# Split weight blocks 544 bytes apart, with three buffer pairs at three places mod 256

## The chip, the cores and the metric

The kernel runs on one core of one Trainium2 chip. The metric is the device time in microseconds of one execution, as the median of several runs. The profile is one further execution, recorded by the hardware profiler; its span is the time from the first to the last instruction.

## What is computed

One step of a layer of a hybrid decoder, for 1024 prompt tokens and 8 sample tokens (1032 columns) and a width of 2048, in float32. Cut to what matters:

```python
h = rmsnorm(x, g_pre)
proj = h @ w_in                                   # 2048 x 10240
q, k, v, za, ub, zb, ga, gb = split(proj)
ya = (retention(q, k, v) * silu(za)) @ w_pa
yb = s5(ub); yb = yb * sigmoid(yb @ w_glu + b_glu)
yb = (yb * silu(zb)) @ w_pb
out = (sigmoid(ga) * ya + sigmoid(gb) * yb) @ w_out
return x + rmsnorm(out, g_post), states
```

Nearly all of the arithmetic is in the products with `w_in`, `w_pa`, `w_pb`, `w_glu` and `w_out`.

## The kernel before

**Split operands.** Both operands of the large products are float32 and are split into a high and a low part of type float32r: high is a cast on ScalarE, low is what the cast left over, a subtraction on VectorE. A product of two split operands is three matmuls: high by high, high by low, low by high (weight named first). Function `three` does this in the first stage, `product` (line 924) in the others.

**Products.** After the first stage the large products are done by a scheme with seven products of half-size blocks instead of eight. A step is one pair of output rows; its seven products use sums and differences of weight blocks (`prep`) and of moving blocks (the forms, which are made earlier and laid into the tiles `a0` to `a15`). One product has four pieces i = 0 to 3 of 128 contraction rows. In the stages up to the output, a moving piece has 516 columns, taken as 256 and 260, so a product is 4 pieces x 3 terms x 2 = 24 matmuls. In the two output stages (`o0`, `o1`) the piece has 324 columns and a product 12 matmuls. There are 90 steps with 24 matmuls a product and 16 steps with 12.

**The stages in order.** First the columns for the S5 branch and the first rows of v, by `linear` and `three`, with moving slices of 384 and 264 columns (lines 218 to 220); then the steps over `w_in`, with the S5 branch and the retention as background work on the other engines; then `glu`, `pa`, `pb`, `o0`, `o1`; last the first 384 tokens of the output product in a form where the weights are the moving operand, 512 columns wide (line 1755).

**Buffers of the split weights.** `wpair` hands out three pairs of buffers in turn, (`whia`, `wloa`), (`whib`, `wlob`), (`whic`, `wloc`). Each is a tile of 520 float32 words, 2080 bytes, of which 512 words are used: four blocks of 128 columns, 512 bytes apart. `prep(g + 2)` casts and subtracts the weights of the product after the next (lines 905 and 85), then the 24 matmuls of product g follow. The pair is free again when the product that used it has ended, so ScalarE waits for TensorE before each cast.

**Places.** A matmul's weight block and its moving piece each start at some byte of a partition. As the pools are laid out, the starts of the tiles mod 256 are:

| tile | start mod 256 before |
|---|---|
| whib, wlob | 160, 192 |
| whic, wloc | 224, 0 |
| whia, wloa | 32, 64 |
| a0, a1, a2, a3, ... | 96, 160, 224, 32, ... (8256 bytes each, 64 mod 256) |

In a moving tile (`qslot`) piece i has its high part at 4128 x (i mod 2) bytes and its low part 2064 bytes behind, so from piece to piece the start moves by 32 mod 256, also across two tiles, and the low part is 16 above the high one. The weight block moves by 512 bytes from piece to piece, 0 mod 256. With the form number the start of the first moving piece alternates between 96 and 224. In the output stages the pieces are 2592 bytes apart and the low part 1296 behind, again 32 and 16 mod 256.

**Smaller tiles that the change touches.** `rms_bcast` (line 269) spreads a row of factors over all partitions by matmuls with a 128x128 tile of ones. `s5_toep` and `s5_states` use small tiles from a pool (`dti`, and `x1` with two buffers). `ret_const` has a tile `selr`, `head` a tile `ons`.

Of the kernel before, what the change touches and what calls it, by code (L numbers as in the profile page):

```python
# [10 lines left out]
F32 = mybir.dt.float32  # L11
F32R = mybir.dt.float32r
I32 = mybir.dt.int32
AF = mybir.ActivationFunctionType
ALU = mybir.AluOpType
# [3 lines left out]
D = 2048  # L19
SEQ = 1024  # L20
NB = 8
# [58 lines left out]
def emit(ctx, tc, I, O):  # L80
    nc = tc.nc
    V, A, P, T = nc.vector, nc.scalar, nc.gpsimd, nc.tensor
# [12 lines left out]

    const = ctx.enter_context(tc.tile_pool(name="const", bufs=1))
    wp = ctx.enter_context(tc.tile_pool(name="wp", bufs=3))
    stage_of = {}

    def stage_pool(w, bufs):  # L100
# [53 lines left out]
        A.dma_start(t, I[name] if src is None else src)  # L154
        return t

    ones = const.tile([128, 128], F32, name="ones")
    onesk = const.tile([128, 1], F32, name="onesk")
    V.memset(onesk, 1.0 / D)
    V.memset(ones, 1.0)  # L160
    rstd = const.tile([128, TOK], F32, name="rstd")
    warm = const.tile([128, 1], F32, name="warm")
    A.activation(warm, onesk, AF.Square)
# [1 line left out]
    ident = cload("ident", [128, 128])  # L165
# [27 lines left out]
        return wtile(wd[m, :, 4 * kq:4 * kq + 4, :])  # L193

    pair_n = [0]

    def wpair():
        n = pair_n[0] = (pair_n[0] + 1) % 3
        return [wp.tile([128, 520], F32R, name=f"{x}{'abc'[n]}", bufs=1)[:, 0:512].rearrange("p (a b) -> p a b", a=4)
                for x in ("whi", "wlo")]  # L200

    def wtile(src):
        turn[0] += 1
        n = turn[0] % (3 + len(more))
        if "pool" in raw_of:
            raw = raw_of["pool"].tile([128, 4, 128], F32, name="wr")
        else:
            raw = more[n] if n < len(more) else wp.tile([128, 4, 128], F32, name="wraw")
        anchor["s"] = nc.sync.dma_start(raw if len(src.shape) == 3 else raw.rearrange("p a b -> p (a b)"), src).ins
        hi, lo = wpair()  # L210
        anchor["a"] = A.copy(hi, raw).ins
        anchor["v"] = sub(lo, raw, hi.bitcast(F32)).ins
        return hi, lo
# [55 lines left out]
    def rms_bcast(ssq, out, pool, extra=None):  # L269
        n = out.shape[-1]  # L270
        chunks = [(c, min(c + 128, n)) for c in range(0, n, 128)]
        nch = len(chunks)
        ps = misc()
        for i, (a, b) in enumerate(chunks):
            T.matmul(ps[0:b - a, i:i + 1], ssq[:, a:b], onesk, start=True, stop=extra is None)
            if extra is not None:
                T.matmul(ps[0:b - a, i:i + 1], extra[:, a:b], onesk, start=False, stop=True)
        ms = pool.tile([128, 9], F32, name="ms")
        rs = pool.tile([128, 9], F32, name="rs")
        hf = pool.tile([128, 9], F32, name="hf")  # L280
        V.memset(ms, 1.0)
        V.memset(hf, -0.5)
        r = chunks[-1][1] - chunks[-1][0]
        full = nch if r == 128 else nch - 1
        V.tensor_scalar(ms[:, 0:full], ps[:, 0:full], EPS, None, ALU.add)
        if full < nch:
            V.tensor_scalar(ms[0:r, full:nch], ps[0:r, full:nch], EPS, None, ALU.add)
        P.tensor_tensor(rs[:, 0:nch], ms[:, 0:nch], hf[:, 0:nch], ALU.pow)
        yield
        for i in range(0, nch, 4):  # L290
            pb = misc()
            for jj in range(i, min(i + 4, nch)):
                a, b = chunks[jj]
                r = b - a
                dg = st_tile()[:, 0:128]
                V.tensor_scalar(dg[0:r, 0:r], ident[0:r, 0:r], rs[0:r, jj:jj + 1], None, ALU.mult)
                T.matmul(pb[:, a - i * 128:b - i * 128], ones[0:r, :], dg[0:r, 0:r], start=True, stop=True)
            a, b = chunks[i][0], chunks[min(i + 4, nch) - 1][1]
            V.tensor_copy(out[:, a:b], pb[:, 0:b - a])

# [98 lines left out]
    def s5_params():  # L399
# [114 lines left out]
        for i in range(10):  # L514
            if i:
# [17 lines left out]


    FIXED = {"E": (14, 0), "rt": (14, 512), "W1": (14, 1024), "Tm": (14, 1536), "mA": (15, 0), "mB": (15, 576),
             "Z": (15, 1088), "zz": (15, 1632), "b2": (15, 1744), "B2": (15, 1808), "bt": (15, 1872), "cp": (15, 1936)}
    whole = {}

    def W(name, shape, bufs=1):
# [115 lines left out]
    def s5_states(b):  # L655
        g0 = 4 * b
        q0 = 2 * b
        pp = s5p
        d = s5d[b]
        W1, U, E, rt = d["W1"], d["U"], d["E"], d["rt"]  # L660
        X = d["X"] = W("X", [128, 4, 137])
        P.dma_start(X[:, :, 0:8], I["x0s"][:, g0:g0 + 4, :])
        P.memset(X[:, :, 8:9], 0.0)
        x0 = W("x0", [128, 2, 2, NB], 2)
        P.dma_start(x0, I["x0p"][:, :, q0:q0 + 2, :])
        Vc = W("Vc", [128, 2, 2, 144])
        for e in range(2):
            ps = misc()
            for q in range(2):
                g = 2 * q + e  # L670
                T.matmul(ps[:, q * 144:(q + 1) * 144], W1[:, g, :], U[:, g, :], start=True, stop=True)  # L671
            pv = ps[:, 0:288].rearrange("p (q c) -> p q c", q=2)
            A.copy(Vc[64 * e:64 * e + 64, 0], pv[0:64])
            A.copy(Vc[64 * e:64 * e + 64, 1], pv[64:128])
        v = Vc[:, :, :, 8:136]
        Erb = E[:, 0:1].broadcast_to([128, 2, 2, 128])
        Eib = E[:, 1:2].broadcast_to([128, 2, 2, 128])
        mA = W("mA", [128, 2, 2, 128])
        mB = W("mB", [128, 2, 2, 128])
        Z = W("Z", [128, 2, 2, 128])  # L680
        fl = lambda t: t.rearrange("p r q c -> p (r q c)")
        yield
        mul(mA, v, Erb)
        mul(mB, v, Eib)
        add(mA[:, 0], mA[:, 0], mB[:, 1])
        sub(mA[:, 1], mA[:, 1], mB[:, 0])
        V.tensor_tensor_scan(fl(Z), fl(rt), fl(mA), 0.0, op0=ALU.mult, op1=ALU.add)
        yield
        mul(mA, Z, Erb)
        mul(mB, Z, Eib)  # L690
        Xv = X.rearrange("p (q e) c -> p e q c", e=2)
        for e in range(2):
            h_ = slice(64 * e, 64 * e + 64)
            sub(Xv[0:64, e, :, 9:137], mA[h_, 0], mB[h_, 1])
            add(Xv[64:128, e, :, 9:137], mA[h_, 1], mB[h_, 0])
        P.tensor_copy(pp["fin"][:, g0:g0 + 4], X[:, :, 136])
        yield

        ab = pp["ar"][:, q0:q0 + 2].unsqueeze(1).unsqueeze(3).broadcast_to([128, 2, 2, NB])
        bb = pp["ai"][:, q0:q0 + 2].unsqueeze(1).unsqueeze(3).broadcast_to([128, 2, 2, NB])  # L700
        x1 = W("x1", [128, 2, 2, NB], 2)
        w2 = W("sw2", [128, 2, 2, NB])
        mul(x1, x0, ab)
        mul(w2, x0, bb)
        sub(x1[:, 0], x1[:, 0], w2[:, 1])
        add(x1[:, 1], x1[:, 1], w2[:, 0])
        add(x1, x1, Vc[:, :, :, 136:144])
        P.dma_start(O["s5s"][:, :, q0:q0 + 2, :], x1)
# [330 lines left out]
    def ret_const():  # L1039
        K["a"] = act.tile([128, 2, TOK], F32, name="a12")  # L1040
        K["b"] = act.tile([128, 2, TOK], F32, name="a13")
        vT, kT = K["next"] = R("vT", [128, TOK]), R("kT", [128, TOK], 2)
        P.dma_start(vT, v_d[0])
        yield
        for n, shape in (("col", [128, 4, H]), ("mask", [128, 128])):
            K[n] = rp.tile(shape, F32, name=n)
            P.dma_start(K[n], I[n])
        K["mhalf"] = rp.tile([128, 8], F32, name="mhalf")
        V.memset(K["mhalf"], -0.5)
        selr = rp.tile([128, 64], F32, name="selr")  # L1050
        P.dma_start(selr, I["sel"])
        K["sel"] = rp.tile([128, 8, 8], F32R, name="sel")
        for a in range(2):
            yield
            P.dma_start(kT[64 * a:64 * a + 64], kq_d[0, 0, a, 0:64])
        yield
        V.tensor_copy(K["sel"], selr.rearrange("p (b c) -> p b c", b=8))
        yield

    R = lambda name, shape, bufs=1, dt=F32: rp.tile(shape, dt, name=name, bufs=bufs)  # L1060
# [8 lines left out]
    def head(h):  # L1069
# [74 lines left out]
        for i in range(2):  # L1144
# [4 lines left out]
                    T.matmul(ps[0:8, 0:128], sel[:, 4 * i + b, :], hl[:, e, b, :], start=i + b + e == 0, stop=i == 1 and b == 3 and e == 1)  # L1149
            if i == 0:  # L1150
                yield
        ons = R("ons", [8, 128])
        A.copy(ons, ps[0:8, 0:128])
        za = qT
        P.dma_start(za, sza_d[h])
# [499 lines left out]
    wb = {}  # L1655

    def next_w():
        gk = order_w.popleft()
        if gk in ((3, 11), (3, 12)):
            raw = wst.tile([128, 4, 128], F32, name="wr").rearrange("p a b -> p (a b)")  # L1660
            hi, lo = (flat(0, "w", F32R)[:, b:b + 512] for b in (1024 * gk[1] - 11264, 1024 * gk[1] - 10752))
            anchor["s"] = nc.sync.dma_start(raw, I["w_outB"][gk]).ins
            anchor["a"] = A.copy(hi, raw).ins
            anchor["v"] = sub(lo, raw, hi.bitcast(F32)).ins
            wb[gk] = hi, lo
        else:
            wb[gk] = [t.rearrange("p a b -> p (a b)") for t in wtile(I["w_outB"][gk])]

    SG = 2 * NP
    SA, SB, SO, SP = SG + 4, SG + 12, SG + 20, SG + 28  # L1670
# [181 lines left out]
```

## Time and profile before

| | |
|---|---|
| median of 3 runs | 2562.95 us (2561.0 to 2564.02) |
| profiled execution, time | 2561.65 us |
| its span | 2559.1 us |
| mean granted TensorE clock | 0.999 |
| busy: TensorE matmuls, weight loads | 2532.5 us, 2486.0 us |
| busy: VectorE, ScalarE, GpSimd | 1996.9 us, 971.4 us, 763.4 us |

PE is the matmul side of TensorE and PEld its weight loads, which overlap the matmuls; DVE is VectorE, ACT ScalarE, POOL GpSimd, SP SyncE. A row of a group gives the line, engine, operation, output and inputs by the program's names, shapes and count, then busy time and the mean ns of one, then the idle time before it and what ended it. A row of the timeline gives the start in us from the span's start, the time to the end of the last one in the row, and how many instructions the row merges; only the first shape of a row is shown, so "128x256 x4" stands for two of 256 and two of 260 columns. A row by windows gives the stretch and its length, then busy time and count of PE, PEld, DVE, ACT and POOL, the granted clock, the DMA share and GB/s.

### The profile page before, as it was taken

What the parts mean: (1) busy time and instruction counts of PE and PEld (TensorE: products, weight loads), DVE (VectorE), ACT (ScalarE), POOL (GpSimd) and SP (SyncE); (2) the same over time, 40 slices, a digit from 0 to 9 for tenths busy, and PEclk for the clock granted to TensorE, in tenths of its full rate; (3) what the DMA queues carried; (4) which work ended last, traced back from release to release, by engine and by line L of the source; (5) the groups of instructions that cost most, each with busy time, mean ns of one, the idle gap of its engine ahead of it and who ended that gap; (6) DMA issues with size and microseconds to landing.
All of it is one profiled execution on the core that took longest, in us unless ns stands there. A gap on an engine that the chain in (4) does not pass through costs nothing.

```text
span 2559.1 us, 52524 instructions
## 1 busy us (share of the span) xinstructions
PE 2532.5 (99%) x19948; PEld 2486.0 (97%) x19948; DVE 1996.9 (78%) x4183; ACT 971.4 (38%) x1747; POOL 763.4 (30%) x1276
## 2 busy tenths in 40 slices
PE   9999999999999999999999999999999999999998
PEld 8999999999999999999999999999999999999876
DVE  7655988898898887557987667667897878989784
ACT  7113223333233334343334444444552432445532
POOL 0103222222222222333334444434332222433320
PEclk9999999999999999999999999999999999999999
DMA  5886434434444447887879888888888689857884
GB/s 196 262 264 216 156 122 123 134 122 132 129 123 127 124 128 245 199 215 198 209 191 246 231 218 227 202 225 236 275 287 281 222 236 316 296 188 168 212 297 134
DMA packets 233500, 519.09 MB, mean 203 GB/s; under 512 B 33968, under 2 KB 61056, under 8 KB 232480
## 3 DMA queue, kind: packets, MB, share of 16 engines
q0 software_dynamic: 103008, 301.75, 41.7%
q1 hardware_dynamic: 91552, 159.30, 19.8%
q10 hardware_dynamic: 38688, 54.70, 6.7%
q8 instruction: 157, 2.57, 0.4%
q14 instruction: 95, 0.78, 0.1%
HBM read 342.36 MB, written 173.25 MB: 201 GB/s over the span
## 4 chain that ended last, share of the span: by engine, by line
PE 90%; DVE 4%; issue 3%; DMA 2%; POOL 1%; ACT 1%; DVEq 0%; POOLq 0%; ACTq 0%
PE acc L924 71%; PE acc L1755 5%; PE mm L220 3%; PE mm L218 3%; PE mm L219 3%; DVE a L85 1%; PE misc L643 1%; PE misc L721 1%; PE misc L720 1%; PE misc L1135 1%; PE misc L1125 1%; PE misc L1104 1%; DVE u L85 1%; PE misc L671 1%; PE misc L1137 0%
## 5 line engine op out<-in xcount | busy, mean ns | idle before, releaser
L924 PE MATMUL acc<-a,whib 128*128 128x256 f32 (+1 forms) x3656 | 607.0, 285 | 2.3 <-DVE u L85 2.2
L924 PE MATMUL acc<-a,whia 128*128 128x256 f32 (+1 forms) x3656 | 607.2, 285 | 1.7 <-DVE u L85 1.2
L924 PE MATMUL acc<-a,whic 128*128 128x256 f32 (+1 forms) x3664 | 606.9, 285 | 1.2 <-ACT whib L905 0.6
L924 PEld LDWEIGHTS acc<-a,whib 128*128 128x128 f32 x3656 | 508.8, 188 | 6.5 <-ACT whia L905 2.4
L924 PEld LDWEIGHTS acc<-a,whia 128*128 128x128 f32 x3656 | 509.6, 188 | 3.2 <-issue 1.9
L924 PEld LDWEIGHTS acc<-a,whic 128*128 128x128 f32 x3664 | 507.3, 188 | 2.0 <-ACT whib L905 0.8
L924 PE MATMUL acc<-a,wloa 128*128 128x256 f32 (+2 forms) x1828 | 383.4, 284 | 0.0
L924 PE MATMUL acc<-a,wloc 128*128 128x256 f32 (+2 forms) x1832 | 382.8, 283 | 0.4 <-DVE wloc L85 0.4
L924 PE MATMUL acc<-a,wlob 128*128 128x256 f32 (+2 forms) x1828 | 382.8, 284 | 0.0
L924 PEld LDWEIGHTS acc<-a,wloc 128*128 128x128 f32 x1832 | 286.5, 188 | 1.2 <-DVE wloc L85 1.2
L924 PEld LDWEIGHTS acc<-a,wloa 128*128 128x128 f32 x1828 | 286.3, 188 | 0.0
L924 PEld LDWEIGHTS acc<-a,wlob 128*128 128x128 f32 x1828 | 286.0, 188 | 0.2
L905 ACT CAST whib<-wraw 128x512 fp32r<-128x512 f32 x140 | 87.0, 621 | 232.0 <-PE acc L924 181.5
L905 ACT CAST whia<-wraw 128x512 fp32r<-128x512 f32 x142 | 88.1, 620 | 226.8 <-PE acc L924 170.9
L905 ACT CAST whic<-wraw 128x512 fp32r<-128x512 f32 x142 | 88.1, 621 | 213.8 <-PE acc L924 163.2
L85 DVE TENSOR_TENSOR wloa<-wraw,whia 128x512 fp32r<-128x512 f32 x152 | 104.2, 686 | 64.0 <-ACT whia L905 37.3
L85 DVE TENSOR_TENSOR wlob<-wraw,whib 128x512 fp32r<-128x512 f32 x151 | 103.5, 685 | 59.1 <-ACT whib L905 39.4
L85 DVE TENSOR_TENSOR wraw<-wr 128x512 f32<-128x512 f32 x212 | 145.3, 686 | 2.6
L905 ACT CAST whib<-wr 128x512 fp32r<-128x512 f32 x107 | 66.4, 620 | 191.2 <-PE acc L924 169.1
L85 DVE TENSOR_TENSOR wloc<-wraw,whic 128x512 fp32r<-128x512 f32 x153 | 104.8, 685 | 43.8 <-ACT whic L905 29.2
L905 ACT CAST whic<-wr 128x512 fp32r<-128x512 f32 x106 | 65.7, 620 | 190.9 <-PE acc L924 167.8
L905 ACT CAST whia<-wr 128x512 fp32r<-128x512 f32 x105 | 65.1, 620 | 189.3 <-PE acc L924 172.1
(457 smaller groups left out, 4575.8 us busy)
## 6 DMA issues: line engine op xcount, KB each, us to landing
wr<-in_w_in SPq DMA_DIRECT2D x280, 256.0 KB
pt_d<-u POOLq DMA_DIRECT2D x70, 258.0 KB, 3.3
u<-pt_d POOLq DMA_DIRECT2D x70, 258.0 KB, 5.0
wr<-in_w_out SPq DMA_DIRECT2D x64, 256.0 KB
wr<-in_w_outB SPq DMA_DIRECT2D x64, 256.0 KB
stg<-fm_d POOLq DMA_DIRECT2D x44, 258.0 KB, 4.3
pt_d<-st POOLq DMA_DIRECT2D x35, 258.0 KB, 3.3
pt_d<-p POOLq DMA_DIRECT2D x35, 258.0 KB, 2.9
```

The lines of the kernel that those rows point to most:

```text
L85: return (eng or V).tensor_tensor(out, a, b, op)
L218: T.matmul(ps, wh[:, i, :], xh[:, t0:t1], start=first, stop=False)
L219: T.matmul(ps, wh[:, i, :], xl[:, t0:t1], start=False, stop=False)
L220: anchor["p"] = T.matmul(ps, wl[:, i, :], xh[:, t0:t1], start=False, stop=last).ins
L643: T.matmul(ps[0:16, g * 128:(g + 1) * 128], B1[:, g, :], W3[:, g, 0:8, :], start=True, stop=True)
L671: T.matmul(ps[:, q * 144:(q + 1) * 144], W1[:, g, :], U[:, g, :], start=True, stop=True)
L720: T.matmul(o, Tm[:, g, :], U[:, g, 0:136], start=True, stop=False)
L721: T.matmul(o, W3[:, g, 1:9, :], X[:, g, 0:136], start=False, stop=True)
L905: anchor["a"] = A.copy(hi, f).ins
L924: anchor["p"] = T.matmul(o, a[:, i, :], x, start=first and i == 0 and a is wh and b is xh, stop=n in (2, 5, 6) and i == 3 and a is wl, ski ...
L1104: T.matmul(ps[:, c * 128:(c + 1) * 128], kt[:, 4 * i + c, :], vt[:, 4 * i + c, :], start=True, stop=True)
L1755: anchor["p"] = T.matmul(ps[c], a, b, start=k == 0 and a is xh and b is wh, stop=k == KD - 1 and a is xl).ins
```

## The change

1. The four blocks of a split weight lie 544 bytes apart instead of 512 (`wblocks`), so the weight's start moves by 32 mod 256 from piece to piece, as the moving piece's does.
2. The six buffers come from two pools, one for the high and one for the low parts, with sizes of 552, 552 and 560 words. The starts mod 256 become: `whi1` and `wlo1` 160, `whi2` and `wlo2` 64, `whi0` and `wlo0` 0. High and low part of a pair are at the same place.
3. The moving tiles start at 160, 224, 32, 96, ... mod 256, since what lies before them has another size.
4. The weights of the last stage, which are moving operands there, stay 512 words in a row at the start of the buffer (`wpair(0)`).
5. To make room, the tile of ones goes (the matmul reads the column `onesk`, 1/2048, broadcast over 128 columns, and the diagonal is multiplied by 2048 in the same instruction), `dti` moves into a part of tile `a15`, `x1` has one buffer, `selr` uses the buffer of `ktS`, and `ons` that of `vs`.

In each product, the start of the moving piece minus that of the weight block, mod 256, was r0, r0+32, r0+64, r0+96 for the four pieces before (high by high). It is the same for all four pieces now: 0 or 128 with pair 1, 96 or 224 with pair 2, 160 or 32 with pair 0, by the parity of the form. The number of instructions and their order on each engine are the same, but for one memset on VectorE that goes.

```diff
     wp = ctx.enter_context(tc.tile_pool(name="wp", bufs=3))
+    wph = ctx.enter_context(tc.tile_pool(name="wph", bufs=1))
+    wpl = ctx.enter_context(tc.tile_pool(name="wpl", bufs=1))
...
-    ones = const.tile([128, 128], F32, name="ones")
...
-    V.memset(ones, 1.0)
...
-    def wpair():
+    WS = (552, 552, 560)
+
+    def wblocks(t):
+        return t[:, 0:544].rearrange("p (a b) -> p a b", a=4)[:, :, 0:128]
+
+    def wpair(flat_at=None):
         n = pair_n[0] = (pair_n[0] + 1) % 3
-        return [wp.tile([128, 520], F32R, name=f"{x}{'abc'[n]}", bufs=1)[:, 0:512].rearrange("p (a b) -> p a b", a=4)
-                for x in ("whi", "wlo")]
+        hi, lo = (p_.tile([128, WS[n]], F32R, name=f"{x}{n}", bufs=1) for p_, x in ((wph, "whi"), (wpl, "wlo")))
+        if flat_at is None:
+            return wblocks(hi), wblocks(lo)
+        return hi[:, flat_at:flat_at + 512], lo[:, flat_at:flat_at + 512]
...
-        hi, lo = wpair()
+        hi, lo = wpair(None if len(src.shape) == 3 else 0)
+        if len(src.shape) == 2:
+            raw = raw.rearrange("p a b -> p (a b)")
...
-                V.tensor_scalar(dg[0:r, 0:r], ident[0:r, 0:r], rs[0:r, jj:jj + 1], None, ALU.mult)
-                T.matmul(pb[:, a - i * 128:b - i * 128], ones[0:r, :], dg[0:r, 0:r], start=True, stop=True)
+                V.tensor_scalar(dg[0:r, 0:r], ident[0:r, 0:r], rs[0:r, jj:jj + 1], float(D), ALU.mult, ALU.mult)
+                T.matmul(pb[:, a - i * 128:b - i * 128], onesk[0:r, :].broadcast_to([r, 128]), dg[0:r, 0:r], start=True, stop=True)
...
-             "Z": (15, 1088), "zz": (15, 1632), "b2": (15, 1744), "B2": (15, 1808), "bt": (15, 1872), "cp": (15, 1936)}
+             "Z": (15, 1088), "zz": (15, 1632), "b2": (15, 1744), "B2": (15, 1808), "bt": (15, 1872), "cp": (15, 1936), "dti": (15, 2000)}
...
-        x1 = W("x1", [128, 2, 2, NB], 2)
+        x1 = W("x1", [128, 2, 2, NB])
...
-        selr = rp.tile([128, 64], F32, name="selr")
+        selr = R("ktS", [128, 64])
...
-        ons = R("ons", [8, 128])
+        ons = R("vs", [8, 128])
...
-            wb[gk] = [t.rearrange("p a b -> p (a b)") for t in wtile(I["w_outB"][gk])]
+            wb[gk] = wtile(I["w_outB"][gk])
```

## The prediction, as it was recorded

> **What bounds the kernel now.** I began with the page's share of busy time by engine and with its chain of waits.
>
> ```profile
> span 2559.1 us, 52524 instructions
> PE 2532.5 (99%) x19948; PEld 2486.0 (97%) x19948; DVE 1996.9 (78%) x4183; ACT 971.4 (38%) x1747; POOL 763.4 (30%) x1276
> PE 90%; DVE 4%; issue 3%; DMA 2%; POOL 1%; ACT 1%; DVEq 0%; POOLq 0%; ACTq 0%
> PE acc L924 71%; PE acc L1755 5%; PE mm L220 3%; PE mm L218 3%; PE mm L219 3%; DVE a L85 1%; PE misc L643 1%; PE misc L721 1%; PE misc L720 1%; PE misc L1135 1%; PE misc L1125 1%; PE misc L1104 1%; DVE u L85 1%; PE misc L671 1%; PE misc L1137 0%
> ```
>
> TensorE is busy 2532.5 of 2559.1 us, so 26.6 us are all that waits can give back. The view of waits, for TensorE alone, says the same; these are its two longest.
>
> ```profile
> PE mm L218 <- ACT whib L211: 5.7, 1, 5.7
> PE acc L924 <- DVE u L85: 3.4, 5, 2.2
> ```
>
> So the kernel is a stream of matmuls, most of them at line 924, and the time is their number times their spacing. The page's groups give the number.
>
> ```profile
> L924 PE MATMUL acc<-a,whib 128*128 128x256 f32 (+1 forms) x3656 | 607.0, 285 | 2.3 <-DVE u L85 2.2
> L924 PE MATMUL acc<-a,whia 128*128 128x256 f32 (+1 forms) x3656 | 607.2, 285 | 1.7 <-DVE u L85 1.2
> L924 PE MATMUL acc<-a,whic 128*128 128x256 f32 (+1 forms) x3664 | 606.9, 285 | 1.2 <-ACT whib L905 0.6
> L924 PEld LDWEIGHTS acc<-a,whib 128*128 128x128 f32 x3656 | 508.8, 188 | 6.5 <-ACT whia L905 2.4
> ```
>
> The high blocks take part in 3656 + 3656 + 3664 = 10976 matmuls and the low ones in half as many, 5488: 16464 in all. Of these, 112 products of the two output stages have 12 matmuls each (1344); the other 15120 form 630 products of 24 matmuls. The mean of 285 ns is latency and not spacing, since matmuls overlap. Each matmul has its own weight load of 188 ns, which runs while the matmul before it streams. For the spacing I took a stretch in which TensorE never waits, in the view by windows.
>
> ```profile
> 957.20:1350.00 392.80, 392.80 (x3314) 392.80 (x3313) 288.93 (x457) 152.75 (x254) 125.11 (x187) 1.00 0.79 209
> ```
>
> The granted clock is 1.00 and 392.80 us hold 3314 matmuls: 118.5 ns each, 2.845 us for a product of 24. Nothing outside TensorE limits this stretch. What can still differ between two products is where their operands lie. The timeline of TensorE shows that this does matter. Each row is a group of matmuls with one operand; a product is four blocks, and each block is a row of a high weight (x4) and a row of its low weight (x2). I quote the starts of products and of the blocks used below, and the end of the last.
>
> ```profile
> 1014.11 0.64 PE L924 MATMUL acc<-a,whic 128*128 128x256 f32 x4
> ...
> 1015.54 0.63 PE L924 MATMUL acc<-a,whic 128*128 128x256 f32 x4
> ...
> 1016.24 0.64 PE L924 MATMUL acc<-a,whic 128*128 128x256 f32 x4
> ...
> 1016.95 0.65 PE L924 MATMUL acc<-a,whia 128*128 128x256 f32 x4
> 1017.44 0.41 PE L924 MATMUL acc<-a,wloa 128*128 128x256 f32 x2
> 1017.69 0.64 PE L924 MATMUL acc<-a,whia 128*128 128x256 f32 x4
> ...
> 1019.83 0.64 PE L924 MATMUL acc<-a,whib 128*128 128x256 f32 x4
> ...
> 1020.54 0.64 PE L924 MATMUL acc<-a,whib 128*128 128x256 f32 x4
> ...
> 1022.67 0.63 PE L924 MATMUL acc<-a,whic 128*128 128x256 f32 x4
> 1023.14 0.40 PE L924 MATMUL acc<-a,wloc 128*128 128x256 f32 x2
> 1023.37 0.64 PE L924 MATMUL acc<-a,whic 128*128 128x256 f32 x4
> ...
> 1024.08 0.63 PE L924 MATMUL acc<-a,whic 128*128 128x256 f32 x4
> ...
> 1024.78 0.63 PE L924 MATMUL acc<-a,whic 128*128 128x256 f32 x4
> ...
> 1025.48 0.63 PE L924 MATMUL acc<-a,whia 128*128 128x256 f32 x4
> ...
> 1026.19 0.63 PE L924 MATMUL acc<-a,whia 128*128 128x256 f32 x4
> ...
> 1028.32 0.64 PE L924 MATMUL acc<-a,whib 128*128 128x256 f32 x4
> ...
> 1029.03 0.64 PE L924 MATMUL acc<-a,whib 128*128 128x256 f32 x4
> ...
> 1031.17 0.40 PE L924 MATMUL acc<-a,whic 128*128 128x256 f32 x2
> ```
>
> Six products in a row, the same 24 matmuls in shape, no wait at any: 2.84, 2.88, 2.84, 2.81, 2.84 and 2.85 us (1014.11 to 1016.95, to 1019.83, to 1022.67, to 1025.48, to 1028.32, to 1031.17). Between the second and the fourth lie 0.07 us, 2.5%. They differ in the buffer pair and in the parity of the form, that is in the place r: start of the moving piece minus start of the weight block, mod 256. A product of the kernel before walks through four places, r0, r0+32, r0+64, r0+96. The six start at r0 = 128, 192, 192, 0, 64, 64. Together they hold each of the eight multiples of 32 three times.
>
> Here the Trainium skill speaks against the change: in "SBUF — State Buffer", section "Who interferes with whom", TensorE has two independent read ports, one for the moving operand and one for weight loads, and never waits on anyone. By that the place could not matter, and the time would stay at 2562.95. The rows of 2.81 and 2.88 us do not agree with it.
>
> **The change, part by part.**
>
> *Places held within a product.* Weight blocks now step by 544 bytes, 32 mod 256, as the moving pieces do (4128 bytes), so all four blocks of a product have one r. The high weights of the three pairs lie at 160, 64 and 0, the moving tiles from 160 on in steps of 64, so r0 takes six values: 0, 128, 96, 224, 160, 32, each for 105 of the 630 products. The places 64 and 192 are no longer visited. What these cost now is read from the rows: at r = 64 the blocks 1024.08 to 1024.78, 1025.48 to 1026.19, 1028.32 to 1029.03 (0.70, 0.71, 0.71); at r = 192 the blocks 1015.54 to 1016.24, 1016.95 to 1017.69, 1019.83 to 1020.54 (0.70, 0.74, 0.71). Their sum is 4.27. All 24 blocks take 17.06 us, 0.7108 each; the 18 that stay in use take 12.79, 0.7106 each. The difference, 0.0003 us, on 630 x 4 = 2520 blocks gives -0.7 us. With starts read to 0.01 us this is zero within some 5 us.
>
> *History.* A block's time is not set by r alone: three blocks at r = 192 took 0.70, 0.74 and 0.71. What came before it counts, and the change alters that everywhere: a product no longer moves on by 32 at each block, it stays. The bound is from both sides. If all blocks ran as the fastest product, 2.81 / 4 = 0.7025, this gives (0.7025 - 0.7108) x 2520 = -21 us; if all ran as the slowest, 2.88 / 4 = 0.72, +23 us. As six kinds of product are drawn anew, and each now repeats one place, the errors do not average out over eight places as before. The six blocks quoted have a spread of 0.015; a mean of six such has 0.006, or 15 us; without the one of 0.74, 0.005 and 0.002, or 5 us. I take 10 us as the uncertainty, between these, and zero as the value, as no row favours staying or moving.
>
> *Low weights.* They lay 32 above the high ones and now lie at the same place mod 256, so the third product term changes place too. The low rows take 0.25 us (1017.44 to 1017.69) and 0.23 us (1023.14 to 1023.37): at most 0.02 x 2520 = 50 us either way if all went from one to the other, about zero if they are spread as now. It is part of the same draw and I do not add it twice.
>
> *Writing four blocks apart.* The cast on ScalarE and the subtraction on VectorE, one of each for a pair, now write four runs of 128 instead of one of 512.
>
> ```profile
> L905 ACT CAST whic<-wraw 128x512 fp32r<-128x512 f32 x142 | 88.1, 621 | 213.8 <-PE acc L924 163.2 <-issue 33.5 <-DVE wraw L85 5.8
> L1274 ACT COPY yo<-yr 128x512 f32<-128x512 f32 x16 | 18.3, 1141 | 0.0
> L85 DVE TENSOR_TENSOR a<-a,a 128x512 f32<-128x512 f32 x32 | 20.9, 685 | 0.2
> L85 DVE TENSOR_TENSOR a<-Vc,a 128x512 f32<-128x512 f32 x32 | 20.6, 685 | 1.3 <-ACT Vc L674 1.3
> 1016.92 0.62 ACT L905 CAST whic<-wraw 128x512 fp32r<-128x512 f32 x1 [0.45 <-PE acc L924]
> ```
>
> On VectorE an operand read in four runs (Vc) costs what a whole one does, 685 ns. On ScalarE the nearest rows are the cast now, 621 ns, and a copy that changes the order of single elements, 1141 ns; I take 621, as runs of 128 are nearer to one run. What hides it: the pair written from 1016.92 is first used at 1022.67, 5.75 us later, and needs 0.62 + 0.69 us. Even at 1141 ns some 3.9 us of cover are left, and ScalarE would go from 971 to about 1300 us. Cost: nothing. If the cover were gone, each cast would add up to 0.5 us.
>
> *The other stages.* Lines 218 to 220 and 1755, and the 1344 matmuls of the output stages, use the new places as well. They are about a quarter of the time; at the spread of 2.5% between products and with the same averaging, +/-3 us, value zero.
>
> *Space.* A memset of 128x128 goes, the row sums' matmuls take a broadcast column as weight, `dti`, `selr`, `ons` and `x1` share or lose a buffer. The order of work on TensorE, ScalarE, POOL and SP is the same, on VectorE it lacks only the memset. Their new waits are for work that ended a stage or a batch earlier, and TensorE's 26.6 us of idle time hold no row of theirs. The few broadcast weight loads are hidden as other loads are; if one were to show, it would cost the 188 ns of a load. Value zero.
>
> **Sum.** The profiled execution took 2561.65 us (span 2559.1 and 2.55 around it), 1.3 below the median of three, 2562.95. With -0.7 it becomes 2560.9; on the median's level 2562.
>
> **Rivals.**
>
> *Faster, holding a place locks loads and streams into a good rhythm.* For it: the fourth product, which spends its blocks at r = 0 to 96, runs at 2.81, and blocks of 0.70 are common. Against it: 160 and 128 are kept, and r = 64, now dropped, is among the good ones. If half of the way to 0.70 is gained on every block, (0.7108 - 0.7054) x 2520 = 14 us: 2549. The full way is 2536.
>
> *Slower, one or two kinds lock into a bad rhythm.* For it: the block at 1016.95 shows that 0.74 exists, and a product that stays would pay it four times where it pays it once now. One kind is 105 x 4 = 420 blocks: (0.74 - 0.7108) x 420 = +12 us, 2574; two kinds 2587. It decides, against 0.2%, once one kind exceeds the mean by 5.1 / 420 = 0.012 us a block.
>
> *The change does nothing for the stream,* the rule of separate ports or a plain average: 2562 to 2563, inside the forecast.
>
> **How the numbers follow.** 0.2% of the time is 5.1 us, about what a measurement of this kernel can tell from no change. A draw around -0.7 with 10 us would leave some 40% within that and the rest nearly even. Faster has 0.34: blocks of 0.70 are seen at several places, and a locked rhythm can keep them. Slower has 0.28, nearly all from the bad rhythm (0.26), 0.02 from the writes on ScalarE and VectorE. No change, 0.38, is the likeliest single case and gives the time, with its own range of 2557 to 2568. The range for all is 10 us x 1.3 on each side and the stages' 3 us, and reaches to the middle of the faster case: 2545 to 2576.
>
> **What would show it.** In the timeline after, a product's four blocks should take equal times, and products of one kind should be alike; six kinds with means of 2.81 to 2.88 us and a mean of about 2.845 bear out the sum. Their mean at 2.82 or less is the first rival, one kind at 2.95 or so the second. Products all alike would bear out separate ports. Wrong would be: waits of TensorE on `whi` or `wlo` beyond the few us of now, or casts much over 621 ns with TensorE idle behind them.

## The result and the profile after

The changed kernel takes 2569.2 us (median of 11 runs, 2565.94 to 2572.42) and the kernel before 2562.95 us (2561.0 to 2565.69) beside it: a ratio of 1.0021, 95% interval 1.0012 to 1.003. It is slower by 6.2 us. That lies inside the forecast range, but the forecast was no change. The profiled execution after took 2569.3 us.

The page of the changed kernel, its busy times and its chain of waits:

```profile
span 2567.1 us, 52530 instructions
PE 2541.3 (99%) x19948; PEld 2493.4 (97%) x19948; DVE 1997.2 (78%) x4182; ACT 972.1 (38%) x1747; POOL 763.6 (30%) x1276
PE 89%; issue 5%; DVE 3%; POOL 2%; DMA 1%; ACT 0%; POOLq 0%; DVEq 0%; SPq 0%; ACTq 0%
```

TensorE has the same 19948 matmuls and is busy 8.8 us longer (2541.3 after 2532.5). What is left of the span is 25.8 us, against 26.6 before. So no new wait has come; the same stream of matmuls flows more slowly. Not all of the 8.8 us is the stream: in this one profiled execution the granted clock is 0.91 from 2420 to 2440 us, some 1.8 us, where the kernel before has 1.00 from 2412 to 2432 us. Two views exclude the costs beside it. First, the longest waits of TensorE in the changed kernel:

```profile
PE mm L226 <- ACT whi L219: 5.1, 1, 5.1
PE acc L1763 <- ACT whi L219: 2.8, 1, 2.8
```

Second, its groups for the cast and for the subtraction, which now write four runs of 128 columns 544 bytes apart:

```profile
L913 ACT CAST whi<-wraw 128x512 fp32r<-128x512 f32 x424 | 263.2, 621 | 675.2 <-PE acc L932 500.2
L85 DVE TENSOR_TENSOR wlo<-wraw,whi 128x512 fp32r<-128x512 f32 x456 | 312.7, 686 | 166.2 <-ACT whi L913 106.8
```

The cast still takes 621 ns, and the subtraction 686 ns after 685 to 686. The loss is in the stream. The stretch without waits that the prediction used shows it in one row of the view by windows, after:

```profile
957.20:1350.00 392.80, 392.80 (x3303) 392.80 (x3302) 288.68 (x457) 150.67 (x251) 123.06 (x185) 1.00 0.79 208
```

Before, 3314 matmuls went through these 392.80 us; now 3303 do, at the same granted clock. That is 118.92 ns each in place of 118.53, and 0.39 ns on the 15120 matmuls of the 24-matmul products is 6.0 us: nearly all of the loss in one number. The first stage adds 1 us or so: 775 matmuls in place of 781 in its first 130 us, at 0.17 us each. Before, then after:

```profile
0.00:130.00 130.00, 124.03 (x781) 122.61 (x782) 86.58 (x126) 51.68 (x65) 11.65 (x34) 1.00 0.71 230
0.00:130.00 130.00, 124.69 (x775) 122.34 (x776) 86.65 (x125) 51.78 (x65) 12.50 (x35) 1.00 0.71 229
```

That this 1 us comes from the places is not shown. The kernel with the space edits alone, told below, has its weights at the old places and also 775 matmuls there; its first product starts at 240.3 us, against 239.3 before and 240.8 after.

Last, the timeline of TensorE after. The rows are the start of a product held at 96 with its four blocks, and then the starts of the next five products and the end of the last:

```profile
1017.37 0.64 PE L932 MATMUL acc<-a,whi 128*128 128x256 f32 x4
...
1018.09 0.65 PE L932 MATMUL acc<-a,whi 128*128 128x256 f32 x4
...
1018.81 0.65 PE L932 MATMUL acc<-a,whi 128*128 128x256 f32 x4
...
1019.53 0.65 PE L932 MATMUL acc<-a,whi 128*128 128x256 f32 x4
...
1020.25 0.63 PE L932 MATMUL acc<-a,whi 128*128 128x256 f32 x4
...
1023.09 0.64 PE L932 MATMUL acc<-a,whi 128*128 128x256 f32 x4
...
1025.94 0.64 PE L932 MATMUL acc<-a,whi 128*128 128x256 f32 x4
...
1028.79 0.64 PE L932 MATMUL acc<-a,whi 128*128 128x256 f32 x4
...
1031.65 0.65 PE L932 MATMUL acc<-a,whi 128*128 128x256 f32 x4
...
1034.51 0.64 PE L932 MATMUL acc<-a,whi 128*128 128x256 f32 x4
```

The product at 96 takes 2.88 us, 0.72 a block. The next, at 32, 0, 224, 160 and 128, take 2.84, 2.85, 2.85, 2.86 and 2.86. The six kinds together take 17.14 us; the six products of before that the prediction read took 17.06. The product of 2.81 that stood there has no successor, and the mean of the six kinds is 2.857 and not about 2.845.

### The profile page after: what moved, and what is told of

It is laid out like the page before. It is cut to its first block, busy times and chain, and to the rows that moved or that the text cites. A ratio compares the mean times of both kernels' runs of the same rounds, so it can differ in the third digit from the quotient of the medians.

```text
span 2567.1 us, 52530 instructions
## 1 busy us (share of the span) xinstructions
PE 2541.3 (99%) x19948; PEld 2493.4 (97%) x19948; DVE 1997.2 (78%) x4182; ACT 972.1 (38%) x1747; POOL 763.6 (30%) x1276
## 4 chain that ended last, share of the span: by engine, by line
PE 89%; issue 5%; DVE 3%; POOL 2%; DMA 1%; ACT 0%; POOLq 0%; DVEq 0%; SPq 0%; ACTq 0%
PE acc L932 69%; PE acc L1763 5%; PE mm L226 3%; PE mm L228 3%; PE mm L227 3%; DVE a L85 1%; PE misc L651 1%; PE misc L729 1%; PE misc L728 1%; PE misc L1133 1%; PE misc L1143 1%; PE misc L1112 1%; PE misc L679 1%; DMA stg<-fo_d 1%; POOL zr L1582 1%
## 5 line engine op out<-in xcount | busy, mean ns | idle before, releaser
L932 PE MATMUL acc<-a,whi 128*128 128x256 f32 (+1 forms) x10976 | 1823.7, 285 | 4.5 <-DVE u L85 2.4
L932 PEld LDWEIGHTS acc<-a,whi 128*128 128x128 f32 x10976 | 1528.6, 188 | 10.7 <-ACT whi L913 4.2
L932 PE MATMUL acc<-a,wlo 128*128 128x256 f32 (+1 forms) x5488 | 1148.1, 284 | 0.4 <-DVE wlo L85 0.4
L932 PEld LDWEIGHTS acc<-a,wlo 128*128 128x128 f32 x5488 | 861.5, 188 | 1.4 <-DVE wlo L85 1.2
L913 ACT CAST whi<-wraw 128x512 fp32r<-128x512 f32 x424 | 263.2, 621 | 675.2 <-PE acc L932 500.2
L85 DVE TENSOR_TENSOR wlo<-wraw,whi 128x512 fp32r<-128x512 f32 x456 | 312.7, 686 | 166.2 <-ACT whi L913 106.8
L913 ACT CAST whi<-wr 128x512 fp32r<-128x512 f32 x318 | 197.4, 621 | 576.4 <-PE acc L932 482.8
L85 DVE TENSOR_TENSOR wlo<-wr,whi 128x512 fp32r<-128x512 f32 x380 | 260.8, 686 | 71.7 <-ACT whi L913 39.5
L226 PE MATMUL mm<-a,whi 128*128 128x384 f32 (+1 forms) x448 | 145.1, 326 | 5.3 <-ACT whi L219 5.1
L228 PE MATMUL mm<-a,wlo 128*128 128x384 f32 (+1 forms) x448 | 145.4, 325 | 0.0
L227 PE MATMUL mm<-a,whi 128*128 128x384 f32 (+1 forms) x448 | 145.3, 324 | 0.0
L85 DVE TENSOR_TENSOR u<-p,acc 128x516 f32<-128x516 f32 (+1 forms) x106 | 69.7, 658 | 27.5 <-issue 11.4
```

What stands on the lines that cost most here:

```text
L85: return (eng or V).tensor_tensor(out, a, b, op)
L226: T.matmul(ps, wh[:, i, :], xh[:, t0:t1], start=first, stop=False)
L227: T.matmul(ps, wh[:, i, :], xl[:, t0:t1], start=False, stop=False)
L228: anchor["p"] = T.matmul(ps, wl[:, i, :], xh[:, t0:t1], start=False, stop=last).ins
L913: anchor["a"] = A.copy(hi, f).ins
L932: anchor["p"] = T.matmul(o, a[:, i, :], x, start=first and i == 0 and a is wh and b is xh, stop=n in (2, 5, 6) and i == 3 and a is wl, ski ...
```

## The experiments

Three theories stood at the start. **Place:** the distance r from weight block to moving piece, mod 256, sets the price of a block, and the change leaves out good distances (64, 192). **Held:** staying at one distance costs in itself. **Else:** the space edits, or what they shift. Each run below has one row of the same window, 957.20 to 1350.00, where no matmul waits. From its count N of matmuls the time against before is worked out as 15120 x 392.80 us x (1/N - 1/3314). The measured difference is between the medians of a kernel and of the kernel before in the same group of runs.

### All products at one pair of distances

The buffers become 544 words long, so that the pairs lie 128 apart mod 256, and 0, 8, 16 or 24 words of padding set which two distances all products hold. Everything else is the changed kernel. The edit for 64 and 192:

```diff
-    WS = (552, 552, 560)
+    WS = (544, 544, 576)
...
     wpl = ctx.enter_context(tc.tile_pool(name="wpl", bufs=1))
+    wpad = ctx.enter_context(tc.tile_pool(name="wpad", bufs=1)).tile([128, 16], F32, name="wpad")
```

> The changed kernel with buffers of 544, 544 and 576 words, so that all three pairs lie at 160 or 32 mod 256 and every product is held at place 0 or 128. Theory Place (a product's time is set by the place it is held at): the timeline of the changed kernel gives products held at 0 a time of 2.85 us and at 128 of 2.86; the mean is that of its six kinds, 2.857, so 2569 us. Theory Held (holding any place costs, since slow places no longer alternate with fast ones): 2569. Theory Else (the cost is in the rest of the change: low weights at the high ones' place, writes of four runs, shared small tiles): 2569. All three agree here; the run gives the level of this form.

> As the run at 0 and 128, with 32 bytes of padding ahead of the moving tiles: every product is held at 32 or 160. Place: the changed kernel's products take 2.84 at 32 and 2.86 at 160, 2.852 on average, 0.005 below its mean of 2.857; times 630 products this is 3 us less, 2566. Held and Else: 2569, the same within 2 us as the other three runs of this set.

> As the run at 0 and 128, with 64 bytes of padding: every product is held at 64 or 192, the two places that the change leaves out. Place: in the kernel before, blocks at these places took 0.70 to 0.71 us where the product had begun at another place (the block of 0.74 was a product's first), so a product takes 2.81 to 2.84, 0.02 to 0.045 less than the changed kernel's; times 630 it is 11 to 28 us less, 2541 to 2558, faster than the kernel before. Held: 2569, like the other places. Else: 2569.

> As the run at 0 and 128, with 96 bytes of padding: every product is held at 96 or 224. Place: the changed kernel's products take 2.88 at 96 and 2.84 at 224, 2.861 on average, 0.004 above its mean; times 630 it is 2.7 us more, 2572, and in the timeline the blocks at 96 take 0.72 each. Held and Else: 2569.

The windows, in the order of these four. At 0 and 128:

```profile
957.20:1350.00 392.80, 392.80 (x3313) 392.80 (x3313) 288.25 (x457) 151.43 (x253) 124.28 (x186) 1.00 0.80 209
```

At 32 and 160:

```profile
957.20:1350.00 392.80, 392.80 (x3305) 392.80 (x3305) 288.45 (x457) 150.64 (x251) 124.03 (x186) 1.00 0.79 209
```

At 64 and 192:

```profile
957.20:1350.00 392.80, 392.80 (x3327) 392.80 (x3326) 290.31 (x460) 153.28 (x254) 125.47 (x188) 1.00 0.80 211
```

At 96 and 224:

```profile
957.20:1350.00 392.80, 392.80 (x3293) 392.80 (x3292) 287.93 (x456) 150.73 (x252) 121.44 (x182) 1.00 0.79 208
```

| distances held | matmuls in the window | worked out from them | measured difference | time, ratio and interval |
|---|---|---|---|---|
| 0, 128 | 3313 | +0.5 us | +1.6 us | 2564.2, 1.0006 (0.9997 to 1.0015) |
| 32, 160 | 3305 | +4.9 us | +5.3 us | 2567.94, 1.0021 (1.0012 to 1.003) |
| 64, 192 | 3327 | -7.0 us | -6.2 us | 2556.45, 0.9974 (0.9964 to 0.9984) |
| 96, 224 | 3293 | +11.4 us | +11.1 us | 2573.77, 1.0047 (1.003 to 1.0064), 4 runs |

Place holds: 17 us lie between two kernels that differ in 32 bytes of padding. Held and Else both wanted one time for all four and fall as sole causes. In the timeline of the kernel at 64 and 192, three products at 64 and then two at 192:

```profile
1016.77 0.63 PE L933 MATMUL acc<-a,whi 128*128 128x256 f32 x4
...
1019.59 0.63 PE L933 MATMUL acc<-a,whi 128*128 128x256 f32 x4
...
1022.40 0.63 PE L933 MATMUL acc<-a,whi 128*128 128x256 f32 x4
...
1025.22 0.64 PE L933 MATMUL acc<-a,whi 128*128 128x256 f32 x4
...
1028.08 0.64 PE L933 MATMUL acc<-a,whi 128*128 128x256 f32 x4
...
1030.94 0.63 PE L933 MATMUL acc<-a,whi 128*128 128x256 f32 x4
```

They take 2.82, 2.81, 2.82 and then 2.86, 2.86. So of the two distances that the change leaves out only 64 is good; 2.86 at 192 is above the 2.845 of the kernel before. The weights of the three products at 64 start at 32, 160 and 32 mod 256, which makes no difference. In that of the kernel at 96 and 224, the four blocks of a product at 96, the end of the next product at 96, and that of one at 224:

```profile
1024.07 0.65 PE L933 MATMUL acc<-a,whi 128*128 128x256 f32 x4
...
1024.81 0.64 PE L933 MATMUL acc<-a,whi 128*128 128x256 f32 x4
...
1025.52 0.65 PE L933 MATMUL acc<-a,whi 128*128 128x256 f32 x4
...
1026.25 0.64 PE L933 MATMUL acc<-a,whi 128*128 128x256 f32 x4
...
1026.97 0.65 PE L933 MATMUL acc<-a,whi 128*128 128x256 f32 x4
...
1029.86 0.64 PE L933 MATMUL acc<-a,whi 128*128 128x256 f32 x4
...
1032.71 0.64 PE L933 MATMUL acc<-a,whi 128*128 128x256 f32 x4
```

At 96 the blocks go 0.74, 0.71, 0.73, 0.72 and the products 2.90 and 2.89; at 224 the product takes 2.85. So one distance alone does not set a block's time either: at 96 a held product alternates here and ran at an even 0.72 in the changed kernel.

The mean spacing over the three pairs that the change keeps (3313, 3305, 3293) is 118.90 ns; the changed kernel has 118.92. Over all four pairs it is 118.69, 2.4 us above before. Leaving out 64 and 192 is thus worth 0.21 ns x 15120 = 3.2 us.

### The space edits alone

The kernel before with the fifth part of the change and nothing of the others; the diff is against the kernel before, and only three of its places are shown.

```diff
-    ones = const.tile([128, 128], F32, name="ones")
...
-        x1 = W("x1", [128, 2, 2, NB], 2)
+        x1 = W("x1", [128, 2, 2, NB])
...
-        selr = rp.tile([128, 64], F32, name="selr")
+        selr = R("ktS", [128, 64])
```

> The kernel before with only the change's space edits (the constant of ones, the table dti, x1 in one buffer, the two borrowed tiles); weight blocks stay 512 bytes apart in the old buffers at the old places. Place theory (the spacing of the matmuls is set by the distance mod 256 between moving piece and weight block, so only the blocks' places count): no change, 2563. Rival (the space edits, or what they shift elsewhere, carry the change's loss): 2569.

2563.5 us, ratio 1.0 (0.9991 to 1.0008), and 3315 matmuls in the window:

```profile
957.20:1350.00 392.80, 392.80 (x3315) 392.80 (x3314) 289.01 (x457) 152.03 (x252) 124.85 (x187) 1.00 0.80 210
```

The space edits cost nothing that the runs can tell.

### Blocks 512 apart in the new buffers

```diff
-        return t[:, 0:544].rearrange("p (a b) -> p a b", a=4)[:, :, 0:128]
+        return t[:, 0:512].rearrange("p (a b) -> p a b", a=4)
```

> The changed kernel with its new buffers, starts and space edits, but the four blocks of a buffer 512 bytes apart, so that a product walks over four distances again; over the program each of the eight distances is visited equally often, and the low weights lie at the same distance as the high ones (before: another). Place theory, block by block: the mean of the four held placements, whose product matmuls took 1813.6, 1817.4, 1807.9 and 1822.7 us against 1813.6 before, so +1.8 us, with the changed kernel's first stage +1.6: 2566. Rival Walking (holding a distance through a product costs in itself): 2563. Rival Low (low weights at the distance of the high ones cost what the change lost): 2569.

2566.47 us, ratio 1.0015 (1.0006 to 1.0024), +3.3 us against before:

```profile
957.20:1350.00 392.80, 392.80 (x3308) 392.80 (x3307) 287.96 (x456) 150.77 (x252) 124.28 (x186) 1.00 0.79 209
```

3308 gives +3.2 us. The expectation by Place, 2566, holds: with every distance used equally often the kernel has the mean of the four held ones (118.69 ns; 392.80 / 3308 is 118.74). But the kernel before uses every distance equally often too and has 3314. About half of the change's loss is therefore there before any distance is left out. Two runs looked for it. In the first the low weights are back at 32 bytes above the high ones; the gap that does this moves the moving tiles by 32 bytes too, so each product also enters its walk 32 further on. In the second only the entry is 32 further on. The two differ in the low weights alone:

```diff
+    wgap = ctx.enter_context(tc.tile_pool(name="wgap", bufs=1)).tile([128, 8], F32, name="wgap")   # first run
     wpl = ctx.enter_context(tc.tile_pool(name="wpl", bufs=1))
+    wpad = ctx.enter_context(tc.tile_pool(name="wpad", bufs=1)).tile([128, 8], F32, name="wpad")   # second run
```

> The kernel with blocks 512 apart in the new buffers, with the low weights 32 bytes above the high ones, as the kernel before has them. If the low weights' place against the high ones' is what remained of the loss there (2566.5): back to 2563 or at most 2565 with the first stage. If it is not: 2566.5.

> The kernel with blocks 512 apart in the new buffers, with 32 bytes of padding ahead of the moving tiles: each product starts 32 further on in its walk, and over the program each of the eight distances is still used equally often. If only how often each distance is used counts: 2566.5 again, within 1.5 us. If the order counts (where a product enters, which distance follows which): another time by 2 us or more.

2567.9 us, 1.0016 (1.0007 to 1.0025), and 2567.77 us, 1.0015 (1.0006 to 1.0023). The window of the first, then that of the second:

```profile
957.20:1350.00 392.80, 392.80 (x3306) 392.80 (x3305) 287.94 (x456) 150.69 (x251) 124.03 (x186) 1.00 0.79 209
```

```profile
957.20:1350.00 392.80, 392.80 (x3306) 392.80 (x3305) 288.02 (x456) 150.73 (x251) 124.02 (x186) 1.00 0.79 208
```

Neither is the cause: three kernels that walk in the new buffers have 3306 to 3308. What remains between them and the kernel before is where the pairs start (at 160, 224, 32 before and at 160, 64, 0 after, mod 256). With that go the distances at which products enter their walk (0, 64, 128 and 192 before), the jump from one product to the next, and the places themselves. None of these was tried by itself, and these 3 us stay open.

### The change with the good pair in place of the bad one

```diff
     wpl = ctx.enter_context(tc.tile_pool(name="wpl", bufs=1))
+    wpad = ctx.enter_context(tc.tile_pool(name="wpad", bufs=1)).tile([128, 8], F32, name="wpad")
```

> The changed kernel with 32 bytes of padding ahead of the moving tiles and nothing else: its products then hold 0, 128, 32, 160, 64 and 192 instead of 0, 128, 96, 224, 32 and 160, so the pair 64/192 takes the turn of 96/224. Place theory: the mean of the placements with all products at 0/128, 32/160 and 64/192, whose products cost +0.5, +4.9 and -7.0 us against before (matmul spacing in one waitless stretch, on 15120 matmuls), is -0.5; with +2 of the first stage 2564. If the change's loss is in holding distances or in the low weights' place: 2569 as it was.

2565.44 us, 1.0004 (0.9995 to 1.0013):

```profile
957.20:1350.00 392.80, 392.80 (x3312) 392.80 (x3312) 288.67 (x457) 150.75 (x251) 124.02 (x186) 1.00 0.79 209
```

With 32 bytes of padding the changed kernel goes from +6.2 us to +1.6, no longer told apart from the kernel before, and from 3303 to 3312 matmuls. This is the direct test that the choice of distances matters: 4.6 us by exchanging one pair of them. It is more than the 3.2 us worked out for leaving out 64 and 192, since the exchange also takes out 96 and 224, the worst pair.

### High and low weights at different distances

In the placement at 64 and 192, a gap of 8, 32 or 24 words between the high and the low buffers, with the padding set so that the high ones stay at 64 and 192:

```diff
     wph = ctx.enter_context(tc.tile_pool(name="wph", bufs=1))
+    wgap = ctx.enter_context(tc.tile_pool(name="wgap", bufs=1)).tile([128, 8], F32, name="wgap")
     wpl = ctx.enter_context(tc.tile_pool(name="wpl", bufs=1))
-    wpad = ctx.enter_context(tc.tile_pool(name="wpad", bufs=1)).tile([128, 16], F32, name="wpad")
+    wpad = ctx.enter_context(tc.tile_pool(name="wpad", bufs=1)).tile([128, 8], F32, name="wpad")
```

> The placement at 64 and 192 with the buffers of the low weights alone 32 bytes higher, so that one matmul of three (low weights by high x) goes at 32 and 160. Place theory, each of the three matmuls counting alike: a third of the way from 2556.5 to 2567.9, 2560.3. Rival (only the high weights' place counts): 2556.5. Rival (the low weights' place counts alone): 2567.9.

> The low weights 32 bytes higher than the high ones as in the earlier run of that, with every block and every moving tile of an odd pair where an even one was: 64 and 192 change roles, distances else the same. If only distances count, mod 256: as the earlier run, 2566. Rival (the absolute place or the pairing of tiles and buffers counts): anything more than 3 us away from that.

> High weights at 64 and 192 as in the best placement, low weights 128 bytes higher against them, so that the low ones go at 192 where the high ones go at 64 and the other way round. If each matmul's own distance sets its price and the prices add: each distance is used as often as in the best placement, 2556.5. Rival Together (high and low of a block have to be at the same distance, as 32 bytes apart cost 10 us where 4 were worked out): 2566.

> The same with the low weights 96 bytes higher: high at 64 and 192, low at 224 and 96. Prices that add: a third of the way from 2556.5 to 2573.8, 2562. Rival Together: 2566 or more, and up to 2574 if the low weights' distance alone decides.

The windows in this order; low weights 32 higher:

```profile
957.20:1350.00 392.80, 392.80 (x3307) 392.80 (x3306) 287.82 (x456) 150.94 (x252) 123.66 (x186) 1.00 0.80 209
```

The same with even and odd pairs exchanged (40 words of padding):

```profile
957.20:1350.00 392.80, 392.80 (x3306) 392.80 (x3305) 287.97 (x456) 150.69 (x251) 123.99 (x186) 1.00 0.78 209
```

Low weights 128 higher:

```profile
957.20:1350.00 392.80, 392.80 (x3312) 392.80 (x3311) 288.12 (x457) 151.22 (x252) 123.96 (x186) 1.00 0.78 209
```

Low weights 96 higher:

```profile
957.20:1350.00 392.80, 392.80 (x3314) 392.80 (x3313) 288.88 (x457) 152.02 (x252) 124.53 (x187) 1.00 0.79 209
```

The times are 2566.27 (1.0013, 1.0004 to 1.0021), 2567.38 (1.0016, 1.0007 to 1.0025), 2563.64 (1.0007, 0.9998 to 1.0016) and 2561.81 us (0.9994, 0.9985 to 1.0003). Exchanging even and odd gives the same (3307, 3306). The distances stay those of the run before it, only other products have them; the starts mod 256 of the weights are unchanged and those of the moving tiles shift by 128. So it does not matter which product has which of the two distances, nor a shift by 128; other shifts of both operands were not compared. But the prices do not add: 32 higher was worked out at 2560.3 and took 2566.3; 128 higher uses each distance as often as the placement without a gap and is 4.7 and 7.2 us slower than the two runs of that placement (the second is told below). Only 96 higher came as added up (2562 expected). What a matmul costs depends on its own distance and on how its neighbours' operands lie: in the run at 128 every distance of every kind of matmul occurs as often as without the gap, and only the combination within a block is new.

### A shift by 16, and the best placement again

Every block 16 bytes further into its buffer, in the placement at 64 and 192:

```diff
-        return t[:, 0:544].rearrange("p (a b) -> p a b", a=4)[:, :, 0:128]
+        return t[:, 0:544].rearrange("p (a b) -> p a b", a=4)[:, :, 4:132]
```

> The placement at 64 and 192 with every block 16 bytes further into its buffer: products at 48 and 176. Place theory, smooth in the distance: half way between the placements at 32/160 and 64/192, 2562. Place in steps of 32: 2556.5 or 2567.9. If only the start of the buffer counts and not the block's own address: 2556.5.

> The placement at 64 and 192 once more, beside the others and on whatever chip this is. If its gain is a property of the placement: 2556.5 again, ratio 0.997. If it was that chip or that draw of runs: 2560 or more.

The shift took 2563.14 us, 0.9998 (0.9989 to 1.0006), half way between the placements at 32 and 160 and at 64 and 192. The best placement, run again beside other kernels, took 2558.92 us, 0.9985 (0.9976 to 0.9993), between the two values that its expectation named. Their windows:

```profile
957.20:1350.00 392.80, 392.80 (x3315) 392.80 (x3314) 289.01 (x457) 151.78 (x252) 124.54 (x187) 1.00 0.80 209
```

```profile
957.20:1350.00 392.80, 392.80 (x3326) 392.80 (x3326) 289.61 (x458) 153.35 (x254) 124.89 (x187) 1.00 0.79 211
```

The stream of the best placement is the same as in its first run (3326 and 3327), so its gain belongs to the placement. Both runs of it are faster than both kernels, by 3.8 and 6.2 us against before.

The time of the shift agrees with the smooth theory by luck. Its timeline shows two products at 176, then two at 48, and the end of the last:

```profile
1012.65 0.63 PE L933 MATMUL acc<-a,whi 128*128 128x256 f32 x4
...
1015.48 0.63 PE L933 MATMUL acc<-a,whi 128*128 128x256 f32 x4
...
1018.31 0.64 PE L933 MATMUL acc<-a,whi 128*128 128x256 f32 x4
...
1021.17 0.64 PE L933 MATMUL acc<-a,whi 128*128 128x256 f32 x4
...
1024.02 0.64 PE L933 MATMUL acc<-a,whi 128*128 128x256 f32 x4
```

At 176 they take 2.83 and 2.83, less than at 160 (2.86, in the changed kernel) and at 192 (2.86). At 48 they take 2.86 and 2.85, more than at 32 (2.84, in the changed kernel) and at 64 (2.82). The two deviations cancel in the sum. So the price is not smooth in the distance, and steps of 16 bytes tell things that steps of 32 do not.

## Why the prediction was wrong, point by point

**What bounds the kernel** was right: the time is the number of matmuls times their spacing, and for all sixteen runs that were set against the kernel before, the count in one waitless window gives the difference of the medians within 3 us (within 1.1 us for all but the second run at 64 and 192).

**Places held within a product** is the step that failed. It took the times of single blocks in a walk as the prices of the same distances when they are held, and so booked leaving out 64 and 192 at -0.7 us. The runs give +3.2 us for it. Both sides were misread. The kept distances read 0.7106 us a block and cost 0.7134 held (6 x 118.90 ns); the two left out read 0.7117 and cost 0.7084 held (6 x 118.06 ns). The largest single error is at 96. Its three blocks in the rows of before start at 1024.78, 1026.19 and 1029.03; the rows that end the last two are

```profile
1026.90 0.64 PE L924 MATMUL acc<-a,whia 128*128 128x256 f32 x4
...
1029.74 0.64 PE L924 MATMUL acc<-a,whib 128*128 128x256 f32 x4
```

So they took 0.70, 0.71 and 0.71, among the best, and held in the changed kernel a block at 96 takes 0.72. On 420 blocks that is 5.6 us by these rows. The 0.74 at 192 is not the fault: the three blocks there read 0.717 on average, and held ones take 0.715 (2.86 / 4). Six blocks read to 0.01 us could not carry a difference of some 0.003; the step said itself that it was zero within some 5 us, and then took zero.

**History** was rightly named and bounded, -21 to +23 us: the four placements lie between -6.2 and +11.1. Its value, zero, was not right: walking in the new buffers already costs some 3 us (3308 matmuls after 3314). What makes these is open.

**Low weights** were put at zero as part of the same draw. In the walk that holds: 3306 matmuls with the low weights at the high ones' distance and 3306 with them 32 from it. In a held placement it does not: 32 bytes cost 7 to 10 us against the two runs without them (3327 and 3326 matmuls to 3307).

**Writes four blocks apart** and **space** at nothing were right: 621 and 686 ns, no new wait, and 2563.5 us with the space edits alone. The figure of about 1300 us for ScalarE at 1141 ns a cast leaves out the output stages; with all 742 casts of line 905 it is 1357, and nothing rests on it. **Other stages** within 3 us held: 1.5 us at the start of the first product, of which the space edits alone show 1.0.

**The rivals.** The slower one had the right sign and half of the mechanism: one kind, 96, is the bad one. Its price was off: 0.74 paid four times would have made 2.96 us a product; 2.88 was measured, and 0.74 comes only every other block where it comes at all. The faster one asked for a good rhythm to be kept; it exists at 64, which the change drops. The rule of the Trainium skill, in "SBUF — State Buffer", section "Who interferes with whom", by which the reads of moving operand and weights are independent, would make all placements alike. The measurement decides against that outcome here: 3293 and 3327 matmuls in the same time.

What makes the difference inside the chip, the reads of weights and moving operands or something else, no run here shows. All products at 64 alone were not tried.

## What to carry to other kernels

Where TensorE never waits, count the matmuls in one waitless window: two profiles of one kernel had 3327 and 3326, while the medians of their runs lay 2.5 us apart. Before changing where weights lie, hold all products at one pair of distances after the other: four kernels that differ in padding told good from bad, while single blocks of a walk mix a distance with what came before it. Regularity gained nothing in itself here: the four held placements have a mean of 118.69 ns a matmul and the walk in the new buffers 118.74. What decides is which distances are held, and, in a held placement, how the low weights of a block lie to its high ones.

## What was not expected of the hardware

A product of 24 matmuls of the same shapes takes 2.81 to 2.90 us by how its weight blocks and its moving pieces lie to each other mod 256, with no wait in the way. The price is not smooth: products held at 48 take more than at 32 or 64, and those at 176 less than at 160 or 192. It also depends on how the neighbouring matmuls' operands lie.

The two profiles of the placement at 64 and 192 have the same stream, but spans of 2553.8 and 2557.9 us. The second has a lower granted clock late in the program, in the window from 2412 us; the first run, then the second:

```profile
2412.00:2440.00 28.00, 25.95 (x120) 20.14 (x119) 19.56 (x45) 11.67 (x24) 5.44 (x8) 1.00 0.78 255
```

```profile
2412.00:2440.00 28.00, 25.88 (x114) 20.14 (x113) 15.78 (x37) 10.63 (x22) 4.36 (x6) 0.94 0.77 255
```

1.00 against 0.94 over these 28 us is some 1.7 us. From 2200 to 2220 us the second run has 0.91 where the first has 1.00, another 1.8 us. The two dips together are 3.5 of the 4.1 us between the spans, and they touch neither the window that was counted nor its count.
